# Instance norm on one core: middle units twice as wide, stored in 64 KB rows

## The chip, the core and the metric

The kernel runs on one core of a Trainium2 chip. A core has five engines with a sequencer each: TensorE (PE in the profile), VectorE (DVE), ScalarE (ACT), GpSimd (POOL) and SyncE (SP). SP computes nothing here; it issues DMA transfers. Transfers issued by SP and by ACT go through two queues (q1 and q10 in the profile), and both queues are worked off by the same 16 DMA engines. On-chip memory has 128 partitions. The metric is the device time in microseconds (us) of one execution, as a median of several runs. A trace comes from one profiled execution; its times count from the start of the span.

## The reference

`x` has the shape 4 x 8 x 16 x 256 x 256 in float32 and `gamma` 8 x 16. Each of the 512 channels (4 images times 128 channels) of 256 x 256 values is normalised by itself:

```python
def reference(x, gamma):
    mu = x.mean(axis=(3, 4), keepdims=True)
    var = ((x - mu) ** 2).mean(axis=(3, 4), keepdims=True)
    x_norm = (x - mu) / np.sqrt(var + 1e-5)
    out = x_norm * gamma[None, :, :, None, None]
    return out.astype(np.float32)
```

134.2 MB are read and 134.2 MB are written, each byte once.

## The kernel before

The input, taken as one flat array, is cut into 32 units of 16 channels, numbered 0 to 31. A channel of 65,536 values lies on 8 partitions (S = 8), so a unit is a tile of 128 partitions x 8192 values: 4 MB, 32 KB in each partition, contiguous in DRAM. There are six slots of that size on the chip (`slots`, the tile `xt`), and unit u uses slot u modulo 6.

Setup. VectorE clears a small tile `touch`, and GpSimd stores it over the first 512 bytes of the 16 channels of unit 0's output (line 54), which unit 0's own store overwrites later. GpSimd loads gamma as one row (line 55). The loads of units 0 to 5 are issued at once: units 1 and 3 on ACT's queue, the others on SP's (lines 56 and 57). Sixty NOPs on ACT stand in the source (line 60). GpSimd builds `navg`, a 128 x 128 matrix that holds -1/65536 in 8 x 8 blocks on the diagonal: as a matmul it sums the 8 partitions of each channel and gives the negative mean to all 8 (lines 66 to 76). VectorE and TensorE spread gamma to one column per group of 16 channels (lines 83 to 94), since unit u has the gammas of group u modulo 8.

The loop over the units (lines 105 to 136) is written in order, and every engine works off its own instructions in that order. For each unit: VectorE sums the tile along its rows (line 107), ScalarE sums its squares (line 108, the squares themselves go to `junk`, which nobody reads), TensorE combines both over the partitions of a channel (line 116), then a short chain goes from VectorE (line 117) to ScalarE (the root, line 121) and back to VectorE (reciprocal and gamma, lines 125 and 127). VectorE then normalises the tile in place (line 130). ACT issues the store (line 134), so ACT's next square stands behind that issue. SP issues the load of unit u + 6 into the slot that the store empties (line 136, issued at line 48), and waits for the store to land before it does so.

What sets the order is the two queues and the semaphores alone. The planner keeps the written order. It hands eight semaphores for completed transfers round, in the order in which transfers of both queues are written, so a transfer is issued only once the transfer eight places before it has landed. In the old kernel that made store 27 wait for load 28.

Of the kernel before, what the change touches and what calls it, by code (L numbers as in the profile page):

```python
# [1 line left out]

# [4 lines left out]

F32 = mybir.dt.float32
U8 = mybir.dt.uint8
ALU = mybir.AluOpType  # L10
ACTF = mybir.ActivationFunctionType
AX = mybir.AxisListType


@with_exitstack
def kernel(
    ctx: ExitStack,
    tc: tile.TileContext,
    x: bass.AP,
    gamma: bass.AP,  # L20
    out: bass.AP,
):
    nc = tc.nc
    B, G, C, H, W = x.shape
    P = nc.NUM_PARTITIONS
    HW = H * W
    n_ch = B * G * C
    S = 8
    K = P // S
    F = HW // S  # L30
    U = n_ch // K
    NG = (G * C) // K
    AHEAD = 6
    assert HW % S == 0 and (G * C) % K == 0

    xv = x.rearrange("b g c h w -> (b g c h w)").rearrange("(u p f) -> u p f", p=P, f=F)
    ov = out.rearrange("b g c h w -> (b g c h w)").rearrange("(u p f) -> u p f", p=P, f=F)
    gv = gamma.rearrange("g c -> (g c)")

    data = ctx.enter_context(tc.tile_pool(name="data", bufs=1))  # L40
    singles = ctx.enter_context(tc.tile_pool(name="singles", bufs=1))
    psum = ctx.enter_context(tc.tile_pool(name="psum", bufs=4, space=bass.MemoryType.PSUM))
    ctx.enter_context(tc.manual_schedule())

    slots = [data.tile([P, F], F32, name=f"xt{i}") for i in range(AHEAD)]

    def load(u, queue):
        queue.dma_start(out=slots[u % AHEAD][:], in_=xv[u])  # L48


    g_row = singles.tile([1, G * C], F32, name="g_row")
    touch = singles.tile([16, 128], F32, name="touch")
    nc.vector.memset(touch[:], 0.0)  # L53
    nc.gpsimd.dma_start(out=ov[0][0::S, 0:128], in_=touch[:])  # L54
    nc.gpsimd.dma_start(out=g_row[:], in_=gv[None, :])  # L55
    for u in range(AHEAD):
        load(u, nc.scalar if u in (1, 3) else nc.sync)

    for _ in range(60):
        nc.scalar.nop()  # L60

    eps_t = singles.tile([P, 1], F32, name="eps_t")
    nc.gpsimd.memset(eps_t[:], 1e-5)
    one = singles.tile([1, 1], F32, name="one")
    nc.gpsimd.memset(one[:], 1.0)
    navg = singles.tile([P, K, S], F32, name="navg")
    nc.gpsimd.memset(navg[:], -1.0 / HW)  # L67
    nc.gpsimd.affine_select(  # L68
        out=navg[:], in_=navg[:], pattern=[[-S, K], [0, S]], compare_op=ALU.is_ge,
        fill=0.0, base=0, channel_multiplier=1,  # L70
    )
    nc.gpsimd.affine_select(  # L72
        out=navg[:], in_=navg[:], pattern=[[S, K], [0, S]], compare_op=ALU.is_ge,
        fill=0.0, base=S - 1, channel_multiplier=-1,
    )
    navg_w = navg[:].rearrange("p k s -> p (k s)")
    root_eps = singles.tile([P, 1], F32, name="root_eps")
    nc.scalar.activation(out=root_eps[:], in_=eps_t[:], func=ACTF.Sqrt)  # L78
    g_rep = singles.tile([1, NG, K, S], F32, name="g_rep")
    g_ps = psum.tile([P, NG], F32, name="g_ps", bufs=1)  # L80
    g_col = singles.tile([P, NG], F32, name="g_col")

    nc.vector.tensor_copy(  # L83
        out=g_rep[:],
        in_=g_row[:].rearrange("o (n k) -> o n k", n=NG).unsqueeze(3).to_broadcast([1, NG, K, S]),
    )
    for n in range(NG):
        nc.tensor.matmul(  # L88
            out=g_ps[:, n : n + 1],
            lhsT=g_rep[:, n].rearrange("o k s -> o (k s)"),  # L90
            rhs=one[:],
            start=True, stop=True,
        )
    nc.vector.tensor_copy(out=g_col[:], in_=g_ps[:])  # L94

    junk = singles.tile([P, F], U8, name="junk")

    st = singles.tile([P, U, 2], F32, name="st")
    nvar = singles.tile([P, U], F32, name="nvar")
    std = singles.tile([P, U], F32, name="std")  # L100
    rstd = singles.tile([P, U], F32, name="rstd")
    scale = singles.tile([P, U], F32, name="scale")

    squares = []
    for u in range(U):
        t = slots[u % AHEAD]
        nc.vector.reduce_sum(out=st[:, u, 0:1], in_=t[:], axis=AX.X)  # L107
        square = nc.scalar.activation(  # L108
            out=junk[:], in_=t[:], func=ACTF.Square, accum_out=st[:, u, 1:2],
        )  # L110
        if u:

            tc.declare_no_dep(square.ins, squares[-1].ins, reason="junk, ordered by the root between")
        squares.append(square)
        ps = psum.tile([P, 2], F32, name="ps")
        nc.tensor.matmul(out=ps[:], lhsT=navg_w, rhs=st[:, u], start=True, stop=True)  # L116
        nc.vector.tensor_scalar(  # L117
            out=nvar[:, u : u + 1], in0=ps[:, 0:1], scalar1=ps[:, 0:1],
            scalar2=ps[:, 1:2], op0=ALU.mult, op1=ALU.add,
        )  # L120
        nc.scalar.activation(  # L121
            out=std[:, u : u + 1], in_=nvar[:, u : u + 1], func=ACTF.Sqrt,
            bias=eps_t[:], scale=-1.0,
        )
        nc.vector.reciprocal(out=rstd[:, u : u + 1], in_=std[:, u : u + 1])  # L125
        g = u % NG
        nc.vector.tensor_mul(  # L127
            out=scale[:, u : u + 1], in0=rstd[:, u : u + 1], in1=g_col[:, g : g + 1],
        )
        nc.vector.tensor_scalar(  # L130
            out=t[:], in0=t[:], scalar1=ps[:, 0:1], scalar2=scale[:, u : u + 1],
            op0=ALU.add, op1=ALU.mult,
        )
        nc.scalar.dma_start(out=ov[u], in_=t[:])
        if u + AHEAD < U:
            load(u + AHEAD, nc.sync)


# [1 line left out]
_INS = ['x', 'gamma']  # L140
_OUTS = [((4, 8, 16, 256, 256), 'float32')]


# [23 lines left out]
```

## Time and profile before

| What | Value |
|---|---|
| median of 3 runs | 626.96 us (626.79 to 627.2) |
| span of the profiled execution | 624.9 us |
| first load lands | 22.6 us |
| last load lands | 585.24 us |
| last store issued, landed | 600.32 us, about 623.9 us |
| busy share of VectorE, ScalarE, TensorE | 71%, 38%, 3% |
| moved by DMA | 268.46 MB, mean 430 GB/s |
| steady period of a load and a store | 19.35 us |

The profiled execution has no time of its own beside the span; the three timed runs lie about 2 us above it. A row of busy tenths gives 40 equal slices of the span. A group line gives the line, engine, operation and shapes, then busy time and mean duration in ns of one, then the idle time before it and what ended that. A line of waits gives who waited for whom, the total in us, how often, and the longest. A DMA issue line ends with the median time from issue to landing.

### The profile page before, as it was taken

What the parts mean: (1) busy time and instruction counts of PE and PEld (TensorE: products, weight loads), DVE (VectorE), ACT (ScalarE), POOL (GpSimd) and SP (SyncE); (2) the same over time, 40 slices, a digit from 0 to 9 for tenths busy, and PEclk for the clock granted to TensorE, in tenths of its full rate; (3) what the DMA queues carried; (4) which work ended last, traced back from release to release, by engine and by line L of the source; (5) the groups of instructions that cost most, each with busy time, mean ns of one, the idle gap of its engine ahead of it and who ended that gap; (6) DMA issues with size and microseconds to landing.
All of it is one profiled execution on the core that took longest, in us unless ns stands there. A gap on an engine that the chain in (4) does not pass through costs nothing.

```text
span 624.9 us, 631 instructions
## 1 busy us (share of the span) xinstructions
PE 21.4 (3%) x80; PEld 19.5 (3%) x80; DVE 443.4 (71%) x163; ACT 238.8 (38%) x98; POOL 2.4 (0%) x11
## 2 busy tenths in 40 slices
PE   0200000000000000000000000000000000000000
PEld 0200000000000000000000000000000000000000
DVE  0588999999776687666786767867668676687730
ACT  0444444444443234432344423444224442244400
POOL 1000000000000000000000000000000000000000
DMA  8999999999999999999999999999999999999998
GB/s 370 436 426 430 422 434 436 436 436 437 432 424 433 436 436 424 436 436 434 436 436 432 422 436 436 434 426 436 436 434 436 436 434 419 436 436 434 426 436 369
DMA packets 9282, 268.46 MB, mean 430 GB/s; under 512 B 1072, under 2 KB 1088, under 8 KB 1088
## 3 DMA queue, kind: packets, MB, share of 16 engines
q10 hardware_dynamic: 4896, 142.61, 52.9%
q1 hardware_dynamic: 4320, 125.83, 46.8%
q0 software_dynamic: 64, 0.01, 0.0%
q14 instruction: 2, 0.02, 0.0%
HBM read 134.22 MB, written 134.23 MB: 430 GB/s over the span
## 4 chain that ended last, share of the span: by engine, by line
another core or an unknown queue 61%; DMA 17%; DVE 15%; SPq 1%; PE 1%; issue 0%; ACT 0%
DVE st L107 10%; DMA xt<-in_x_dram 10%; DMA out_dram<-xt 8%; DVE xt L130 5%; SPq L48 1%; PE ps L116 1%; ACT std L121 0%; DVE nvar L117 0%; DVE rstd L125 0%; DVE scale L127 0%
## 5 line engine op out<-in xcount | busy, mean ns | idle before, releaser
L107 DVE TENSOR_REDUCE st<-xt 128x1 f32<-128x8192 f32 x32 | 277.9, 8685 | 100.4 <-DMA xt<-in_x_dram 100.4
L108 ACT ACTIVATE junk<-xt 128x8192 uint8<-128x8192 f32 x32 | 225.0, 7030 | 275.1 <-DMA xt<-in_x_dram 231.9
L130 DVE TENSOR_SCALAR xt<-xt,ps,scale 128x8192 f32<-128x8192 f32 x32 | 145.6, 4550 | 1.2
L121 ACT ACTIVATE std<-nvar,eps_t 128x1 f32<-128x1 f32 x32 | 9.4, 294 | 79.6 <-DVE nvar L117 79.6
L116 PE MATMUL ps<-st,navg 128*128 128x2 f32 x64 | 17.9, 349 | 557.1 <-DVE st L107 557.1
L116 PEld LDWEIGHTS ps<-st,navg 128*128 128x128 f32 x64 | 16.0, 311 | 558.9 <-issue 558.9
L117 DVE TENSOR_SCALAR nvar<-ps 128x1 f32<-128x1 f32 x32 | 9.2, 287 | 23.8 <-PE ps L116 23.8
L125 DVE RECIPROCAL rstd<-std 128x1 f32<-128x1 f32 x32 | 5.2, 164 | 11.6 <-ACT std L121 11.6
L83 DVE COPY g_rep<-g_row 1x1024 f32<-1x1024 f32 x1 | 0.7, 681 | 14.3 <-DMA g_row<-in_gamma_dram 14.3
L108 ACT ACTIVATION_READ_ACCUMULATOR junk<-xt 128x1 f32 x32 | 6.0, 186 | 0.0
L127 DVE TENSOR_TENSOR scale<-rstd,g_col 128x1 f32<-128x1 f32 x32 | 5.1, 159 | 1.1
L88 PE MATMUL g_ps<-one,g_rep 1*128 1x1 f32 x16 | 3.5, 347 | 16.1 <-DVE g_rep L83 16.1
L88 PEld LDWEIGHTS g_ps<-one,g_rep 1*128 1x128 f32 x16 | 3.5, 325 | 16.1 <-issue 16.1
L94 DVE COPY g_col<-g_ps 128x8 f32<-128x8 f32 x1 | 0.2, 166 | 3.7 <-PE g_ps L88 3.7
L78 ACT ACT_TABLE_LOAD x1 | 1.3, 1283 | 1.7 <-PEq L151 1.7
L53 DVE MEMSET touch<- 16x128 f32 x1 | 0.2, 165 | 0.9 <-PEq L151 0.9
L54 POOL DMA_DIRECT2D out_dram<-touch x1 | 0.6, 619 | 0.8 <-DVE touch L53 0.8
L55 POOL DMA_DIRECT2D g_row<-in_gamma_dram x1 | 0.5, 487 | 0.0
L68 POOL TENSOR_SCALAR_AFFINE_SELECT navg<-navg 128x128 f32<-128x128 f32 x1 | 0.4, 400 | 0.1
L72 POOL TENSOR_SCALAR_AFFINE_SELECT navg<-navg 128x128 f32<-128x128 f32 x1 | 0.4, 399 | 0.1
L67 POOL MEMSET navg<- 128x128 f32 x1 | 0.2, 232 | 0.0
L78 ACT ACTIVATE root_eps<-eps_t 128x1 f32<-128x1 f32 x1 | 0.2, 203 | 0.0
(6 smaller groups left out, 0.6 us busy)
## 6 DMA issues: line engine op xcount, KB each, us to landing
out_dram<-xt ACTq DMA_DIRECT2D x32, 4096.0 KB, 62.5
xt<-in_x_dram SPq DMA_DIRECT2D x30, 4096.0 KB, 38.5
xt<-in_x_dram ACTq DMA_DIRECT2D x2, 4096.0 KB, 31.5
out_dram<-touch POOLq DMA_DIRECT2D x1, 8.0 KB, 9.1
g_row<-in_gamma_dram POOLq DMA_DIRECT2D x1, 0.5 KB, 13.3
```

Source lines behind the costliest of these rows:

```text
L48: queue.dma_start(out=slots[u % AHEAD][:], in_=xv[u])
L78: nc.scalar.activation(out=root_eps[:], in_=eps_t[:], func=ACTF.Sqrt)
L83: nc.vector.tensor_copy(out=g_rep[:], in_=g_row[:].rearrange("o (n k) -> o n k", n=NG).unsqueeze(3).to_broadcast([1, NG, K, S]),)
L88: nc.tensor.matmul(out=g_ps[:, n : n + 1], lhsT=g_rep[:, n].rearrange("o k s -> o (k s)"), rhs=one[:], start=True, stop=True,)
L107: nc.vector.reduce_sum(out=st[:, u, 0:1], in_=t[:], axis=AX.X)
L108: square = nc.scalar.activation(out=junk[:], in_=t[:], func=ACTF.Square, accum_out=st[:, u, 1:2],)
L116: nc.tensor.matmul(out=ps[:], lhsT=navg_w, rhs=st[:, u], start=True, stop=True)
L117: nc.vector.tensor_scalar(out=nvar[:, u : u + 1], in0=ps[:, 0:1], scalar1=ps[:, 0:1], scalar2=ps[:, 1:2], op0=ALU.mult, op1=ALU.add,)
L121: nc.scalar.activation(out=std[:, u : u + 1], in_=nvar[:, u : u + 1], func=ACTF.Sqrt, bias=eps_t[:], scale=-1.0,)
L125: nc.vector.reciprocal(out=rstd[:, u : u + 1], in_=std[:, u : u + 1])
L127: nc.vector.tensor_mul(out=scale[:, u : u + 1], in0=rstd[:, u : u + 1], in1=g_col[:, g : g + 1],)
L130: nc.vector.tensor_scalar(out=t[:], in0=t[:], scalar1=ps[:, 0:1], scalar2=scale[:, u : u + 1], op0=ALU.add, op1=ALU.mult,)
```

## The change

The flat array is now cut into 22 units, numbered 0 to 21. The first six and the last six are as before: 16 channels, 8 partitions each, 4 MB. The ten in the middle (units 6 to 15) are wide: 32 channels, 4 partitions each, 128 partitions x 16384 values, 8 MB, 64 KB in each partition. The six slots become three pairs of slots, each pair one tile; a wide unit fills a pair.

A wide unit is loaded by two transfers, one for each half of its columns. Each moves rows of 32 KB that lie 64 KB apart in DRAM, one after the other on SP's queue. Each half is summed and squared when it is there, and the two matmuls add up in one accumulator. The wide unit is normalised by one instruction and stored by one transfer with rows of 64 KB. A list `behind` says which loads are issued behind the store of which unit: unit 6 behind store 1, unit 7 behind store 3, unit 8 behind store 5, each of units 9 to 15 behind the store of the unit three before it, units 16 and 17 behind store 13, 18 and 19 behind store 14, 20 and 21 behind store 15. Each load still waits for the store that held its slot.

For the wide units there is a second averaging matrix (4 x 4 blocks) and a second set of gamma columns, made in the setup. `touch`, its store and the NOPs are gone.

```diff
-    AHEAD = 6
+    SLOTS = 6
+    ENDS = 6
...
-    slots = [data.tile([P, F], F32, name=f"xt{i}") for i in range(AHEAD)]
+    pairs = [data.tile([P, 2, F], F32, name=f"xt{i}") for i in range(SLOTS // 2)]
+    units = []
+    at = 0
+    slot = 0
+    total = n_ch // K
+    while at < total:
+        wide = 2 if ENDS <= at < total - ENDS else 1
+        units.append((at, wide, slot))
+        at += wide
+        slot = (slot + wide) % SLOTS
+    U = len(units)
+
+    def on_chip(u):
+        at, wide, slot = units[u]
+        pair = pairs[slot // 2]
+        if wide == 2:
+            return pair[:].rearrange("p t f -> p (t f)")
+        return pair[:, slot % 2]
+
+    def in_dram(flat, u):
+        at, wide, slot = units[u]
+        return flat[at * K * HW : (at + wide) * K * HW].rearrange("(p f) -> p f", p=P)
 
     def load(u, queue):
-        queue.dma_start(out=slots[u % AHEAD][:], in_=xv[u])
-    touch = singles.tile([16, 128], F32, name="touch")
-    nc.vector.memset(touch[:], 0.0)
-    nc.gpsimd.dma_start(out=ov[0][0::S, 0:128], in_=touch[:])
+        wide = units[u][1]
+        for h in range(wide):
+            queue.dma_start(
+                out=on_chip(u)[:, h * F : (h + 1) * F],
+                in_=in_dram(xf, u)[:, h * F : (h + 1) * F],
+            )
...
+    for u in range(U):
+        free += held[u]
+        while nxt < U and held[nxt] <= free:
+            free -= held[nxt]
+            behind[u].append(nxt)
+            nxt += 1
...
-    for _ in range(60):
-        nc.scalar.nop()
...
+    for wide in (1, 2):
+        s = S // wide
+        k = K * wide
+        ng = GC // k
+        m = singles.tile([P, k, s], F32, name=f"navg{wide}")
...
-        nc.vector.reduce_sum(out=st[:, u, 0:1], in_=t[:], axis=AX.X)
-        square = nc.scalar.activation(
-            out=junk[:], in_=t[:], func=ACTF.Square, accum_out=st[:, u, 1:2],
-        )
+        for h in range(wide):
+            part = t[:, h * F : (h + 1) * F]
+            nc.vector.reduce_sum(out=st[:, u, 2 * h : 2 * h + 1], in_=part, axis=AX.X)
+            square = nc.scalar.activation(
+                out=junk[:], in_=part, func=ACTF.Square, accum_out=st[:, u, 2 * h + 1 : 2 * h + 2],
+            )
...
+            nc.tensor.matmul(
+                out=ps[:], lhsT=navg[wide], rhs=st[:, u, 2 * h : 2 * h + 2],
+                start=h == 0, stop=h == wide - 1,
+            )
...
-        nc.scalar.dma_start(out=ov[u], in_=t[:])
-        if u + AHEAD < U:
-            load(u + AHEAD, nc.sync)
+        nc.scalar.dma_start(out=in_dram(of, u), in_=t)
+        for v in behind[u]:
+            load(v, nc.sync)
```

## The prediction

> **What bounds the kernel now.** I read the page first: the rows over time and the queues.
>
> ```profile
> span 624.9 us, 631 instructions
> DVE  0588999999776687666786767867668676687730
> DMA  8999999999999999999999999999999999999998
> GB/s 370 436 426 430 422 434 436 436 436 437 432 424 433 436 436 424 436 436 434 436 436 432 422 436 436 434 426 436 436 434 436 436 434 419 436 436 434 426 436 369
> DMA packets 9282, 268.46 MB, mean 430 GB/s; under 512 B 1072, under 2 KB 1088, under 8 KB 1088
> q10 hardware_dynamic: 4896, 142.61, 52.9%
> q1 hardware_dynamic: 4320, 125.83, 46.8%
> ```
>
> The DMA row is full from end to end, and the two queues' packets fill 99.7% of the 16 engines' time. VectorE, the busiest engine, stands at 71%. A queue holds 144 packets per transfer of 4 MB (4320 over 30 loads): 128 rows of 32 KB and 16 completions. So a packet here is one row.
>
> Next the waits of the DMA queues, and the DMA issues.
>
> ```profile
> SPq L48 <- DMA out_dram<-xt: 534.4, 26, 59.5
> ...
> out_dram<-xt ACTq DMA_DIRECT2D x32, 4096.0 KB, 62.5
> xt<-in_x_dram SPq DMA_DIRECT2D x30, 4096.0 KB, 38.5
> out_dram<-touch POOLq DMA_DIRECT2D x1, 8.0 KB, 9.1
> g_row<-in_gamma_dram POOLq DMA_DIRECT2D x1, 0.5 KB, 13.3
> ```
>
> SP waits 534 us for stores to free slots, yet always has a second load queued: a load takes 38.5 us from issue to landing, two periods. The small rows matter most: 8 KB took 9.1 us, the time of some seven 32 KB rows. A queue with little to move waits while the other queues' rows pass whole.
>
> Then the chain of waits (start, duration), the store issues over time, and the groups.
>
> ```profile
> 159.62 0.33 SPq L48
> 546.69 0.03 issue
> 546.72 38.51 DMA xt<-in_x_dram
> 585.26 8.70 DVE st L107
> 595.73 4.55 DVE xt L130
> ```
>
> ```profile
> 503.49 0.34 ACTq L134 DMA_DIRECT2D out_dram<-xt  x1
> 527.20 0.34 ACTq L134 DMA_DIRECT2D out_dram<-xt  x1
> 600.32 0.34 ACTq L134 DMA_DIRECT2D out_dram<-xt  x1
> ```
>
> ```profile
> L107 DVE TENSOR_REDUCE st<-xt 128x1 f32<-128x8192 f32 x32 | 277.9, 8685 | 100.4 <-DMA xt<-in_x_dram 100.4
> L108 ACT ACTIVATE junk<-xt 128x8192 uint8<-128x8192 f32 x32 | 225.0, 7030 | 275.1 <-DMA xt<-in_x_dram 231.9
> L130 DVE TENSOR_SCALAR xt<-xt,ps,scale 128x8192 f32<-128x8192 f32 x32 | 145.6, 4550 | 1.2
> ```
>
> Twenty load issues between 159.62 and 546.69 give a period of 19.354 us for a load and a store: 9.677 per transfer, 1.205 per row on each engine and about 0.04 per completion. 64 x 9.677 = 619.3; only 5.6 us of the span are start and end. The last load lands at 585.24, its store is issued 15.08 us later, and all that time stores 28, 29 and 30 (29 us) keep the engines full. That cover is what I watch.
>
> **The change part by part.** The sum goes against the span of 624.9; the median of 626.96 lies 2.06 above it.
>
> Fewer transfers: 22 stores for 32. Ten completions at 0.04: -0.4 us. Whether a 64 KB row is cheaper per byte the trace can't show. Bounds: nothing, or the middle's stores (20 of the 64 transfers) at the best slice's 437 GB/s instead of the period's 8.389 MB / 19.354 us = 433.4: 0.8% of 193.5, -1.6. I take -0.4, since only the completions go away with certainty.
>
> Column halves: a load row is still 32 KB, now 64 KB from the next. Nothing shows this; bounds nothing, and the slowest inner slice (419 against 436, 3.9%) over 20 x 9.677: +7.5. I take nothing, because each row stays one contiguous packet. The Trainium skill, "DMA: Bandwidth & Descriptors", Latency and other measured facts, has copies slowing at large power-of-two pitches (207 GB/s at 512 KiB against 214 full); at 3% the halves would cost an estimated 6 us. No run here shows it, and this pitch is an eighth of that.
>
> Setup: touch and its DMA go. Store 0 waited on it, but it had landed by 10.5 us and the store was issued at 37.68: nothing. Had it warmed the store path, its loss would fall on store 0; stepping through the first rounds below misses the trace by 1.2 us, so +/-1.2, and I take 0. The 60 NOPs have no record, and the table load starts at 1.72, straight behind ACT's two DMA issues: 0. A second averaging matrix costs POOL 1.0 (0.23 + 0.40 + 0.40) at about 4 us, idle time. The second gamma column costs a copy of 0.68, half of L88's 3.5 and a copy of 0.17 behind 19.9 us, so VectorE is free near 22.9 rather than at 22.6: 0.3 late, hidden since store 0 waits behind load 3 on ACT's queue until about 42. Without cover it is 0.3.
>
> Wide units: 32 reductions and 32 squares as before; ten chains of small operations fewer, about 1.75 each on VectorE, which has slack. Normalise: 2 x 4.55 = 9.1. From a second half's landing to its store: 8.70 + 1.75 + 9.1 = 19.6 us instead of 15.1. ACT waits that out with the next square queued behind; squares at 7.2 catch up with reductions at 8.7. SP still has 30 issues, ACT 24 instead of 34. The issues also wait on each other eight back (store 27 was issued 4.4 us late, as load 28 landed); in the schedule below those transfers have landed in time.
>
> **The turn.** A wide store puts rows of 64 KB against loads of 32 KB. If engines take turns by row, stores get two bytes for one of the loads: eight turns of 2.41 + 1.205 = 28.9 us move a whole 8 MB store and only one 4 MB half. Both queues having equal rows, before can't show this directly; by bytes the gap would be nil. I take rows, as the 9.1 us of the 8 KB store is nearest. The Trainium skill, "DMA: Bandwidth & Descriptors", Queues, rings and completion order, says each engine round-robins between queues and finishes a packet before switching. Its typical packet of 9 to 17 descriptors isn't what the trace has (a row each), but with packet equal to row it says the same, and would make turns by bytes wrong.
>
> I stepped the whole schedule by these numbers: data starts 1.3 us after the issue, landing shows 0.95 after the last row, engines alternate, slots free as the diff has it. For the old kernel this gives the last load at 584.0, its store issued at 599.0 and landed at 622.7; the trace has 585.24, 600.32 and 623.9 (600.32 + 23.6). It is 1.2 early throughout. For the new one, unshifted:
>
> - Until 158 nothing differs (stores 4 and 5 land at 138.6 and 158.0). Then wide stores take 31 to 32 us from issue to landing and run ahead of the loads.
> - Wide stores 13, 14 and 15 land at 450.5, 494.0 and 523.0; each releases two of the last six loads.
> - At 523.0 all 26 units of 4 MB before the last six are out, but the rest of load 17 and loads 18 to 21 are still to come. From here rows are equal: they land at 527.9, 544.8, 564.1, 583.5 and 602.9. Each narrow store follows its load by 15.1 and shares with the next.
> - At 602.9 only store 20 is left (issued 598.5, its data ends by 611.7). Store 21 is issued at 602.9 + 15.1 = 618.0 and starts at 619.3: the engines stand idle for 7.6 us. It lands at 602.9 + 15.1 + 1.3 + 9.68 + 0.95 = 629.9.
>
> Against 622.7 that is +7.1 to +7.2, the -0.4 included. Shifting one input at a time (row time, latencies, mid chain by a few tenths) gives +7.1 to +8.4. I take +7.6: span 632.5, time 634.6.
>
> With turns by bytes, store 15 lands at 535.1 with three loads left; they land at 554.5, 573.8 and 593.2. Stores 19 and 20 (19.4 us) then cover 15.1 + 1.3, and the end is 622.3.
>
> **The rivals.**
> - Turns by bytes: -0.4, 626.5. For it: two queues with equal rows share evenly to the last digit. Against: the 8 KB store.
> - The change doesn't do what it says, 64 KB rows being sent as two packets of 32 KB: the same 626.5. For it: every packet so far is at most 32 KB. A wide store would then show 272 packets instead of 144.
> - Faster: 64 KB rows move at the best slice's rate in the middle, -1.6, 625.3. It decides only where the tail stays covered, that is where no more than three loads are left as store 15 lands. Against: stores alone (604 to 622 us) and loads alone (4 to 36 us) run at 430 and 427 GB/s, so neither direction has a faster mode. By the Trainium skill, "DMA: Bandwidth & Descriptors", Specifications, the fabric's ceiling is 435 GB/s; the period's 433.4 agrees and leaves little.
> - The strided halves are slow: up to +7.5 on the forecast, 642. Against: the row length and the packet count are unchanged.
>
> **How the numbers follow.** Turns by row 0.70, by itself 632.0 to 637.5 (7.1 to 8.4, and 1.2 either way for touch and 64 KB rows). Turns by bytes 0.11, split rows 0.09, faster 0.06, slow halves 0.04. A measurement can tell about 0.2% (1.25 us) from no change: faster 0.06, same 0.20, slower 0.74. The range reaches from the two even cases to the top of the likeliest: 626.0 to 637.5; faster and slow halves are left out.
>
> **What would show it.** Right: q10 with 3456 packets (24 x 144); wide stores landing about 31 us after issue and the two halves further apart than their sizes; the last load near 604; a last slice or two of GB/s well below 369 with a gap of 7 to 8 us before the last store. Wrong: last load near 594 and no gap; or middle slices below 430. I would be wrong most simply if the engines share by bytes.

## The result

The changed kernel takes 668.2 us (median of four runs, 664.07 to 670.11) against 626.88 us for the kernel before in the same rounds: a ratio of 1.0649, 95% interval [1.0618, 1.0681]. The forecast was 634.6 with a range of 626.0 to 637.5. The direction was right; the loss is 41 us instead of 8. The changed kernel also scatters by 0.5% either way, the old one by 0.03%. (Where a kernel's runs lie more than 1.5% above its fastest, the ratio leaves them out and the median does not.)

The profiled execution took 666.68 us. The page, for the rows that were shown of before:

```profile
span 665.0 us, 591 instructions
...
DMA  9999999999999999999999999999999999999665
GB/s 378 442 410 432 424 438 442 430 422 426 335 361 347 323 442 452 405 447 416 430 412 396 424 404 428 436 410 386 422 426 442 416 422 396 430 434 440 300 277 252
DMA packets 7811, 268.47 MB, mean 404 GB/s; under 512 B 896, under 2 KB 896, under 8 KB 896
...
q10 hardware_dynamic: 3456, 142.61, 52.2%
q1 hardware_dynamic: 4320, 125.83, 44.8%
```

A slice is 16.6 us. There are three losses: four slices of 323 to 361 GB/s (166 to 233 us) in which the DMA row still says 9, a middle that hovers below the old 433, and three slices of 252 to 300 at the end with the engines partly idle. q10 has the 3456 packets that were forecast for rows sent whole.

The stretches of the trace say the same with sharper edges. Columns: stretch, its length, busy time of each engine with its instructions, granted clock, the share of time in which the DMA engines have a packet, and GB/s. First the kernel before, then the changed one:

```profile
159.00:228.00 69.00, 2.23 (x8) 2.00 (x8) 50.93 (x20) 29.66 (x12) 0.00 (x0) 1.00 1.00 433
228.00:440.00 212.00, 6.13 (x22) 5.51 (x22) 151.84 (x53) 81.29 (x32) 0.00 (x0) 1.00 1.00 434
```

```profile
40.00:158.00 118.00, 4.47 (x16) 4.02 (x16) 101.63 (x32) 56.81 (x22) 0.00 (x0) 1.00 1.00 430
159.00:228.00 69.00, 1.12 (x4) 1.00 (x4) 26.80 (x6) 14.54 (x5) 0.00 (x0) 1.00 1.00 350
228.00:440.00 212.00, 6.14 (x22) 5.52 (x22) 144.21 (x35) 80.11 (x28) 0.00 (x0) 1.00 1.00 423
440.00:634.00 194.00, 5.01 (x18) 4.50 (x18) 130.00 (x38) 66.16 (x25) 0.00 (x0) 1.00 0.95 404
634.00:664.00 30.00, 0.56 (x2) 0.50 (x2) 13.85 (x5) 7.42 (x3) 0.00 (x0) 1.00 0.67 287
```

From 159 to 228 us, while the first two wide stores run, the engines are full (1.00) but move 350 instead of 433 GB/s. So the packets themselves take longer. Only from 440 on is the share below 1.

Issues with the median time to landing, and the end of the chain of waits:

```profile
xt<-in_x_dram SPq DMA_DIRECT2D x30, 4096.0 KB, 52.4
out_dram<-xt ACTq DMA_DIRECT2D x12, 4096.0 KB, 26.9
...
out_dram<-xt ACTq DMA_DIRECT2D x10, 35.6
```

```profile
637.81 8.70 DVE st L159
...
648.28 4.55 DVE xt L183
```

Loads take 52.4 us (38.5 before): the stores run ahead of them, as forecast. The last load lands at 637.81 (585.24 before, forecast near 604), and its store goes out 15.05 us later, at 652.86, after the engines have run dry.

**An account by packets.** The trace also has a record of each packet: queue, start, duration, bytes. The tables below are my own sums over these records. At full speed a row of 32 KB takes 1.213 us and one of 64 KB 2.418. A row's excess is its time above that; the column also holds the completions, 9 ns each on record. All in us for each of the 16 engines, counted from the first data packet (at 1.8 us of the span) to the last:

| | stretch | rows at full speed | slow rows' excess | idle | last load ends at |
|---|---|---|---|---|---|
| before | 621.8 | 621.1 | 1.9 | -1.2 | 581.9 |
| changed | 661.8 | 620.4 | 24.7 | 16.7 | 634.4 |

The loss of 40.0 us is 22.8 of slow rows and 17.9 of idle time, less 0.7 because a row of 64 KB takes 0.3% less than two of 32 KB. Of the slow rows' 24.7, 12.5 are the 64 KB rows of 159 to 228 us alone (241 of the 256 rows of the first two wide stores are slow). Of the idle 16.7, some 9 fall after the last load has landed and some 8 before; 6.6 of these 8 lie between 612.6 us, when the first of the engines lands its part of that load, and 637.8, when the last one does.

### The profile page after: what moved, and what is told of

Same layout as the page of the kernel before. It is cut to its first block, busy times and chain, and to the rows that moved or that the text cites. A ratio compares the mean times of both kernels' runs of the same rounds, so it can differ in the third digit from the quotient of the medians.

```text
span 665.0 us, 591 instructions
## 1 busy us (share of the span) xinstructions
PE 23.3 (3%) x88; PEld 21.3 (3%) x88; DVE 434.0 (65%) x124; ACT 235.9 (35%) x88; POOL 3.1 (0%) x13
## 3 DMA queue, kind: packets, MB, share of 16 engines
q10 hardware_dynamic: 3456, 142.61, 52.2%
## 4 chain that ended last, share of the span: by engine, by line
DVE 41%; DMA 30%; another core or an unknown queue 24%; PE 1%; ACT 1%; issue 1%; SPq 0%
DVE st L159 26%; DMA xt<-in_x_dram 18%; DVE xt L183 14%; DMA out_dram<-xt 12%; PE ps L166 1%; ACT std L174 1%; DVE nvar L170 1%; SPq L73 0%; DVE rstd L178 0%; DVE scale L180 0%
## 5 line engine op out<-in xcount | busy, mean ns | idle before, releaser
L183 DVE TENSOR_SCALAR xt<-xt,ps,scale 128x8192 f32<-128x8192 f32 (+1 forms) x22 | 142.8, 6490 | 0.8
L166 PE MATMUL ps<-st,navg 128*128 128x2 f32 x64 | 17.9, 349 | 612.0 <-DVE st L159 612.0
L174 ACT ACTIVATE std<-nvar,eps_t 128x1 f32<-128x1 f32 x22 | 6.5, 294 | 58.3 <-DVE nvar L170 58.3
L170 DVE TENSOR_SCALAR nvar<-ps 128x1 f32<-128x1 f32 x22 | 6.3, 288 | 16.4 <-PE ps L166 16.4
L178 DVE RECIPROCAL rstd<-std 128x1 f32<-128x1 f32 x22 | 3.6, 164 | 7.9 <-ACT std L174 7.9
L135 PE MATMUL g_ps<-one,g_all 1*128 1x1 f32 x24 | 5.4, 348 | 11.9 <-DVE g_all L130 11.9
L135 PEld LDWEIGHTS g_ps<-one,g_all 1*128 1x128 f32 x24 | 5.3, 324 | 12.0 <-issue 11.3
L180 DVE TENSOR_TENSOR scale<-rstd,g_col 128x1 f32<-128x1 f32 x22 | 3.5, 159 | 0.7
## 6 DMA issues: line engine op xcount, KB each, us to landing
xt<-in_x_dram SPq DMA_DIRECT2D x30, 4096.0 KB, 52.4
```

What stands on the lines that cost most here:

```text
L135: nc.tensor.matmul(out=g_ps[:, n : n + 1], lhsT=g_rep[:, n].rearrange("o k s -> o (k s)"), rhs=one[:], start=True, stop=True,)
L166: nc.tensor.matmul(out=ps[:], lhsT=navg[wide], rhs=st[:, u, 2 * h : 2 * h + 2], start=h == 0, stop=h == wide - 1,)
L170: nc.vector.tensor_scalar(out=nvar[:, u : u + 1], in0=ps[:, 0:1], scalar1=ps[:, 0:1], scalar2=ps[:, 1:2], op0=ALU.mult, op1=ALU.add,)
L174: nc.scalar.activation(out=std[:, u : u + 1], in_=nvar[:, u : u + 1], func=ACTF.Sqrt, bias=eps_t[:], scale=-1.0,)
L180: nc.vector.tensor_mul(out=scale[:, u : u + 1], in0=rstd[:, u : u + 1], in1=g_cols[wide][:, g : g + 1],)
L183: nc.vector.tensor_scalar(out=t, in0=t, scalar1=ps[:, 0:1], scalar2=scale[:, u : u + 1], op0=ALU.add, op1=ALU.mult,)
```

## The experiments

Edits are against the changed kernel unless another is named; "wide" is 2 for a wide unit. The first theory after the result was that something about the wide store's rows is slow in itself: their length, their distance in DRAM, or the strided halves.

**Place and length of the rows.**

```diff
 e1: wide stores in two column halves (32 KB rows, 64 KB apart)
-        nc.scalar.dma_start(out=in_dram(of, u), in_=t)
+        for h in range(wide):
+            nc.scalar.dma_start(
+                out=in_dram(of, u)[:, h * F : (h + 1) * F], in_=t[:, h * F : (h + 1) * F],
+            )
 e2: only the first 60 KB of each wide row, rows 64 KB apart
+            L = 15360
+            nc.scalar.dma_start(out=in_dram(of, u)[:, :L], in_=t[:, :L])
 e3: the same 60 KB, rows 60 KB apart
+            rows = of[at * K * HW : at * K * HW + P * L].rearrange("(p f) -> p f", p=P)
+            nc.scalar.dma_start(out=rows, in_=t[:, :L])
```

> The changed kernel, but a wide unit is stored in two column halves, as it is loaded: rows of 32 KB, 64 KB apart, two transfers. In the changed kernel's trace the first two wide stores (160 to 233 us) have rows of 64 KB that take about 3.2 us instead of 2.42, and the loads beside them pass one 4 MB half per 8 MB store. Theory A (the place: 16 engines writing rows that lie 64 KB apart, in step, are slow whatever the rows' length): store rows of 32 KB over 1.21 us by a third, time 640 to 655. Theory B (the length: a row of 64 KB is what is slow and what takes the longer turn): all rows at 1.21 us, even turns, last load lands near 594, time 626 to 628.

> The changed kernel, but of each 64 KB row of a wide unit only the first 60 KB are stored (a sixteenth of the wide units' output is left out, 5.2 MB or 12 us of DMA); rows still start 64 KB apart. Theory A (place): rows over their share of 2.27 us (60/64 of 2.42) by a third in the first wide stores, time 650 to 660. Theory B (length): the same, 650 to 660. It is the control of the next kernel.

> As the kernel before it in this set, 60 KB of each row of a wide unit stored, but the rows lie 60 KB apart in DRAM, without gaps, so the engines' rows no longer start a power of two apart (the output is at other places, and 12 us of DMA are left out). Theory A (place): rows at 2.27 us, no slow stretch, only the tail of late loads is left: 615 + 8 = 620 to 625. Theory B (length): no different from the kernel with rows 64 KB apart, 650 to 660.

| | time | ratio to before |
|---|---|---|
| e1, stores in halves | 627.66 | 1.0009 [0.9999, 1.0018] |
| e2, 60 KB rows 64 KB apart | 661.41 | 1.0547 [1.0526, 1.0569] |
| e3, 60 KB rows 60 KB apart | 660.88 | 1.0539 [1.0507, 1.0571] |

e1 has the wide units, strided halves in both directions, second matrix, the waits and the missing touch, and is as fast as the kernel before. So all of the loss comes with storing a wide unit as one transfer of 64 KB rows, and the column halves cost nothing. e1 changes two things at once, the length of the rows and the size of the transfer; e5 below takes them apart. e2 and e3 agree: the distance of the rows doesn't matter, and rows that move 6% less of the wide output remain slow.

**Other pairs of row lengths.** In e5 the wide store stays one transfer, each row sent as two pieces of 32 KB. In e6 all pieces are halved (loads and narrow stores 16 KB, wide stores 32 KB). In e7 wide loads are one transfer of 64 KB rows. e9 and e10 are the kernel before with the pieces of one direction cut to 16 KB.

```diff
 e5
+        nc.scalar.dma_start(out=in_dram(of, u), in_=t, max_dma_last_dim=32768)
 e6: also on each load max_dma_last_dim=16384
+        nc.scalar.dma_start(out=in_dram(of, u), in_=t, max_dma_last_dim=16384 * wide)
 e7
+        queue.dma_start(out=on_chip(u), in_=in_dram(xf, u))
 e9, in the kernel before
+        queue.dma_start(out=slots[u % AHEAD][:], in_=xv[u], max_dma_last_dim=16384)
 e10, in the kernel before
+        nc.scalar.dma_start(out=ov[u], in_=t[:], max_dma_last_dim=16384)
```

> The changed kernel with every wide store still one transfer of 8 MB, but sent as two 32 KB pieces per row. Theory B (a piece over 32 KB is what is slow): no slow piece, even turns, the same as with two stores per unit, 626 to 628. If the transfer of 8 MB were the trouble, and not its rows: 660 to 670.

> The changed kernel with every row cut in half: loads and narrow stores in pieces of 16 KB, wide stores in pieces of 32 KB. The turns are as uneven as in the changed kernel (two bytes stored for one loaded while wide stores run), but no piece is over 32 KB. Theory B1 (a piece over 32 KB is slow by itself): pieces at 1.21 and 0.61 us, and only the prediction's step is left, late loads at the end with about 7.6 us of idle engines: 633 to 637. Theory B2 (uneven turns are what slows the stores, whatever the length): wide store pieces a third over 1.21 us, 655 to 670.

> The changed kernel with wide loads in one transfer with rows of 64 KB as well, so turns are even and half a unit is never there early. Theory B1 (over 32 KB is slow by itself): stores, perhaps loads too, over 2.42 us, 650 to 690. Theory B2 (uneven turns): rows at 2.42 us; the late halves alone cost little, 626 to 640.

> The kernel before, narrow units alone, but every load goes in pieces of 16 KB beside stores of 32 KB: uneven turns with nothing else changed. Theory T (turns by piece): two bytes stored for one loaded, loads fall behind, and the same stepping as in the prediction gives 12.4 us of idle engines at the end and 1.5 us for the smaller pieces: 639 to 643. If the engines share by bytes, or the uneven turn only matters with pairs of slots: 626 to 629.

> The mirror image: stores in pieces of 16 KB beside loads of 32 KB, so that loads run ahead and the stores are what is left at the end, when they need nothing but the engines. Theory T: no idle, 1.5 us for the smaller pieces, 627 to 629.5. If uneven turns cost engine time by themselves (stores slowed beside longer rows): 635 or more.

| | store / load piece, KB | time | ratio to before | excess | idle |
|---|---|---|---|---|---|
| e5 | 32 / 32, store of 8 MB | 637.86 | 1.0167 [1.0146, 1.0188] | 7.3 | 5.5 |
| e6 | 32 / 16 in the middle | 652.61 | 1.0369 [1.0311, 1.0427] | 8.8 | 14.0 |
| e7 | 64 / 64 in the middle | 636.99 | 1.0157 [1.0137, 1.0177] | 7.8 | 4.0 |
| e9 | 32 / 16 throughout | 653.14 | 1.0384 [1.0327, 1.0441] | 10.3 | 14.9 |
| e10 | 16 / 32 throughout | 636.22 | 1.0146 [1.0112, 1.0179] | 4.5 | 4.1 |

In e5 the rows have 32 KB and the store is still one of 8 MB: some 30 us of the loss are gone, and some 11 us remain while the transfer stays one of 8 MB. The time lies in neither of its two ranges, and the same holds for e6 and e9; e10 hits the range for uneven turns that cost engine time by themselves, and e7 the one for even turns.

e9 shows the turn by itself, in a kernel without any 64 KB row. Its issues:

```profile
out_dram<-xt ACTq DMA_DIRECT2D x32, 4096.0 KB, 19.8
xt<-in_x_dram SPq DMA_DIRECT2D x30, 4096.0 KB, 79.2
```

Equal transfers of 4 MB, but stores land in 19.8 us and loads in 79.2 (62.5 and 38.5 before): the queue with pieces twice as long runs ahead. It is as slow as e6, with much the same split of excess and idle time. Every combination of pieces that I tried, other than transfers of 4 MB in rows of 32 KB both ways, was slower.

**How many wide units.** One constant.

```diff
 e4: -    ENDS = 6
     +    ENDS = 14     (two wide units)
 e11: -    ENDS = 6
      +    ENDS = 2     (fourteen wide units)
```

> The changed kernel with 14 narrow units at each end, so two wide units only. If each wide store in step costs its slow rows, two of them cost 8 rows x 0.8 us each, some 13 us, and no late loads remain at the end, since 14 narrow units follow: 636 to 642. If the loss comes from late loads behind stores alone (the prediction's tail) nothing is left: 626 to 628.

> The changed kernel with two narrow units at each end instead of six, so 14 wide units. Stepping the schedule gives no late loads at the end (the pairs fall differently): idle near nothing. If the slow rows go by the number of wide stores, 14/10 of 22.8 us is 32: 655 to 662. If the idle stretch at the end comes from engines drifting apart and not from late loads, it stays at 15 us or grows: 670 to 680.

e4 took 650.01 us (1.0366 [1.0299, 1.0432]), e11 655.83 (1.0440 [1.0404, 1.0476]). Stretches of e4, then of e11:

```profile
40.00:314.00 274.00, 8.93 (x32) 8.02 (x32) 212.27 (x72) 116.05 (x46) 0.00 (x0) 1.00 1.00 432
314.00:382.00 68.00, 1.12 (x4) 1.01 (x4) 31.96 (x10) 14.83 (x6) 0.00 (x0) 1.00 1.01 361
382.00:600.00 218.00, 6.13 (x22) 5.50 (x22) 154.70 (x56) 84.00 (x34) 0.00 (x0) 1.00 1.00 429
```

```profile
40.00:190.00 150.00, 5.03 (x18) 4.52 (x18) 112.72 (x29) 63.69 (x23) 0.00 (x0) 1.00 1.00 431
190.00:440.00 250.00, 6.70 (x24) 6.01 (x24) 173.97 (x38) 94.36 (x32) 0.00 (x0) 1.00 1.01 432
440.00:585.00 145.00, 3.91 (x14) 3.51 (x14) 80.56 (x19) 43.62 (x15) 0.00 (x0) 1.00 0.99 413
585.00:602.00 17.00, 0.56 (x2) 0.50 (x2) 8.97 (x2) 7.19 (x3) 0.00 (x0) 1.00 0.37 156
```

Two wide units cost 23 us. 15.6 us an engine are slow rows, 10.0 of them the two wide stores' own: both are slow for nearly their whole length (2.95 and 3.14 us a row), at 314 us instead of 159, so the moment in the kernel is not the cause. The other 5.0 are idle; I had expected none, because my steps for this kernel were wrong, not because of the chip (redone by the forecast's own rules they give an estimated 6 to 8). With fourteen wide units the rows run at 2.42 to 2.48 us and 431 to 432 GB/s for 400 us; I had expected slow rows there; that the time still falls into the range expected for them, 655 to 662, is luck. Its loss is idle time above all (21.1 us of it against 10.0 of slow rows), half of it at 585 to 602, where the engines have a packet for 37% of the time. So "64 KB rows beside 32 KB rows" is not slow as such, and the loss has two parts that come and go separately.

**The row's price without the kernel.** e8 and e12 do nothing but transfers: phases, one after the other, of 32 MB out of one tile and 32 MB into two others, 64 KB or 32 KB rows.

```diff
 e8, phases (store KB, load KB):  32/-  64/-  32/32  64/32  64/64  32/64  32/16
 e12, phases of 64/32: loads from the stores' places; the same, with VectorE
   and ScalarE at work on the stored tile; loads from 24 MB ahead; from 16 MB
   ahead; then 64/- and 32/32 with the engines at work
```

> No normalisation at all: seven phases, one behind the other, each of which stores 32 MB from one tile and, in the last five, loads 32 MB beside it. Rows in KB (store, load): 32 alone; 64 alone; 32 and 32; 64 and 32; 64 and 64; 32 and 64; 32 and 16. Theory B1: store rows of 64 KB take over 2.42 us in all their phases, the alone one too. Theory B2: only where the rows are unequal, that is also 32 beside 16. A third, C: only beside loads, because a long row of one engine stands against other engines' loads; then 64 alone runs at 430 GB/s and 64 beside 32 or 64 does not. By turns by row, 64 beside 32 moves two bytes out for one in, 32 beside 64 one for two.

> Six phases as in the phases before, no normalisation, stores of 64 KB rows beside loads of 32 KB rows: (1) loads and stores at the same offset, (2) the same with VectorE's sums and ScalarE's squares running over the stored tile, (3) loads three units of 8 MB further on than the stores, (4) two further on, as in the changed kernel, (5) 64 KB stores alone with the sums and squares, (6) 32 KB beside 32 KB with them. Theory D1 (compute on the tile slows a long row and throws engines out of step): rows over 2.42 us in phases 2 and 5 alone. Theory D2 (the place of loads against stores in DRAM): phases 3 and 4 alone, at about 3.3 us. Neither: all at 2.42 us.

In e8, 64 KB rows took 2.42 us alone and 2.418 to 2.44 beside 32 KB loads, at 430 GB/s. That phase's 32 MB of stores took 124.7 us from the signal to the last landing, where equal shares of 433 GB/s would need 155: the stores got close to two bytes for each of the loads (524 load rows begun beside 512 store rows of twice the length). VectorE's wait for those stores:

```profile
458.13 0.06 DVE L52 MEMSET src<- 128x1 f32 x1 [124.67 <-DMA out_dram<-src]
```

In e12 the same work as in e8's fourth phase was slow in the first phase and nearly full speed in the second:

```profile
22.00:164.00 142.00, 0.00 (x0) 0.00 (x0) 0.00 (x0) 1.00 0.99 349
209.00:332.00 123.00, 82.33 (x10) 36.90 (x11) 0.00 (x0) 1.00 0.99 417
```

The engines at work (82 and 37 us in the second row) do no harm, and loads from other places (2.55 and 2.68 us a row) lie between the two. Yet the first row's 349 GB/s is all but the 350 of the changed kernel at 159 to 228. Something decides between 2.42 and 3.0 us for the same rows.

**Engines out of step?** In the changed kernel the 16 engines, which land a transfer within 0.4 to 0.5 us of each other until the first wide store, drift 18 us apart by 400 us and up to 43 later. I took that for the cause. e13 puts half of the engines one row behind by a store of 8 rows ahead of phases 3, 5 and 6; e14 puts all behind alike by 16 rows; e15 lets loads and stores go together (phases 1, 3, 5) or 8.7 or 17.4 us apart (2, 4 and 6).

```diff
 e13 (e14: [0:16, 0:F])
+        nc.scalar.dma_start(out=rows(of, 16 - len(kicks))[0:8, 0:F], in_=src[0:8, 0:F])
 e15, between the signal that lets the loads go and that for the stores
+        for _ in range(later):
+            nc.vector.reduce_sum(out=st[:, 0:1], in_=src[:, 0:F], axis=AX.X)
```

> No normalisation: seven phases, one after the other, each with 32 MB out beside 32 MB in; phases 1 to 5 have 64 KB store rows beside 32 KB load rows, phases 6 and 7 have 32 KB both ways. Ahead of phases 3, 5 and 6 stands a store of 8 rows of 32 KB, which should reach only 8 of the 16 engines, one row each, and put them 1.2 us behind the others. Theory (engines out of step slow the long rows, whatever put them out of step): phases 3 and 5 slow, that is four stores in about 140 to 148 us with a mean 64 KB row of 2.8 to 3.1 us; phases without the kick are a matter of how they happen to start, fast (125 us, 2.42 us) where their first rows start within 1 us of each other, slow where not; phases 6 and 7 (equal rows) full speed, 1.21 us a row, about 155 us for both ways, kick or no kick. Rival 1 (the slow state belongs to a place in memory): phases 1 and 4 (same places) are alike, 2 and 5 are alike, whatever the kick. Rival 2 (the slow state is a matter of the moment on the chip): no pattern with the kick.

> As the kernel with the kick of 8 rows, but the store ahead of phases 3, 5 and 6 has 16 rows, one for each engine, so that all engines are put behind alike. Theory: the kick does nothing to the step of the engines, phases 3 and 5 are like phases 1, 2 and 4, fast (125 us, 2.42 us) where the first rows start together; a phase 3 or 5 that is slow here as often as with 8 rows speaks against the theory. Rival 1: as before, by place. Rival 2: no pattern.

> No normalisation: seven phases of 32 MB out beside 32 MB in, phases 1 to 6 with 64 KB store rows beside 32 KB load rows, phase 7 with 32 KB both ways. In phases 1, 3 and 5 loads and stores are let go within half a microsecond, in 2 and 4 the stores one sum of 8.7 us behind the loads, in 6 two sums. In the three phase kernels so far the first phase was slow (3.01 to 3.07 us a 64 KB row, loads and stores 2.3 us apart, the 16 engines in step) and all later ones less so (2.42 to 2.68 us, 5 to 28 us apart). Theory A (loads and stores that begin together run over the same rows and get in each other's way): phases 1, 3 and 5 at 2.9 to 3.1 us, phases 2, 4 and 6 at 2.42 to 2.7. Theory B (what comes first in a kernel is slow): phase 1 alone near 3.0, phases 2 to 6 all at 2.42 to 2.7. Phase 7 at 1.21 to 1.25 by both.

The theory fell, and so did both of e15's. A 64 KB row's mean by phase: e13 3.01, 2.58, 2.67, 2.47, 2.51; e14 3.07, 2.49, 2.47, 2.61, 2.57; so the kicked phases 3 and 5 are not the slow ones. Phases 1 and 4, at the same places, differ by 0.5 us. In e15:

```profile
22.00:164.00 142.00, 0.00 (x0) 0.00 (x0) 1.00 0.99 350
219.00:361.00 142.00, 0.00 (x0) 0.00 (x0) 1.00 0.99 350
395.00:538.00 143.00, 0.00 (x0) 0.00 (x0) 1.00 0.99 350
593.00:734.00 141.00, 0.06 (x1) 0.00 (x0) 1.00 0.99 353
768.00:911.00 143.00, 0.00 (x0) 0.00 (x0) 1.00 0.99 352
974.00:1118.00 144.00, 0.06 (x1) 0.00 (x0) 1.00 0.97 380
```

The first five phases are all slow, with the engines' first rows within 0.4 to 0.65 us of each other: engines in step are slow here. (In the sixth the first rows lie 1.65 us apart, and a row takes 2.74 on average.) In e11 they were in step as well and fast. The pattern that was left is in the order of the rows. A transfer of 128 rows is 8 rows for each engine. I counted, at the start of each store row, how many load rows an engine had begun, less the store rows begun before it: the loads' lead, taken modulo 8. At a lead of 1, an engine loads row r of a transfer just before it stores row r of another. In e15 the phases with a start apart had a lead of 9, which is 1 again.

**The lead, set on purpose.** e16 lets both go together and has 0, 64, 0, 32, 128 and 96 rows loaded first, to set the lead. e18 repeats that with 0, 16 and 112 (phases 1, 4 and 5), and turns the order of the rows in DRAM alone, for the stores in phase 2 and for the loads in phase 3.

```diff
 e16, and e18 in phases 4 and 5
+        if lead:
+            nc.sync.dma_start(
+                out=dst[1][0:lead, F:], in_=rows(xf, 15)[0:lead, F:], max_dma_last_dim=32 * 1024,
+            )
 e18, in phases 2 and 3, for the DRAM side
+        return rows(flat, u).rearrange("(b a) f -> a b f", a=16)
```

> No normalisation: six phases of 32 MB out in rows of 64 KB beside 32 MB in in rows of 32 KB, loads and stores let go within half a microsecond. A transfer is 8 rows for each of the 16 engines. Ahead of the loads of phases 2, 4, 5 and 6 stands one more load of 64, 32, 128 and 96 rows: 4, 2, 8 and 6 rows for each engine, so that the loads run so many rows behind the stores. Theory C (an engine's rows are slow while it loads row number r of its eight between storing row r and r + 1 of the same eight places): phases 1, 3 and 5 (0, 0 and 8 rows apart, the same numbers) at 2.9 to 3.1 us a 64 KB row, phases 2, 4 and 6 at 2.42 to 2.6. In the kernel with starts 8.7 us apart the loads were 12.7 us, about a whole transfer of 8 rows, ahead, and it was slow too, which fits. Theory D (engines that start within 0.65 us of each other are slow, whatever the rows): all six at 2.9 to 3.1. Against D: with two narrow units at each end the engines were in step from 95 to 127 us and every row took 2.42.

> No normalisation: six phases of 32 MB out beside 32 MB in, loads and stores let go together, loads in rows of 32 KB. Phase 1: 64 KB store rows, nothing else. Phase 2: the store's 128 rows go to DRAM in the order 0, 16, 32 ... 112, 1, 17 ...; on the chip they are taken in the same order as in phase 1. Phase 3: the loads' rows are taken from DRAM in that order instead. Phases 4 and 5: as phase 1 with 16 and 112 rows loaded first, one and seven for each engine. Phase 6: 32 KB rows both ways. Theory C with the partitions as the cause (an engine writes partition p on the chip just before it reads partition p): phases 1, 2 and 3 all at 2.9 to 3.1 us a 64 KB row. Theory C with the places in DRAM as the cause: phase 1 at 3.0, phases 2 and 3 at 2.42 to 2.6. By both: phases 4 and 5 (another row number) at 2.42 to 2.55, phase 6 at 1.21 to 1.25.

The phases of e16, while the stores run:

```profile
22.00:166.00 144.00, 0.06 (x1) 0.00 (x0) 1.00 0.99 350
210.00:328.00 118.00, 0.00 (x0) 0.00 (x0) 1.00 0.99 419
377.00:521.00 144.00, 0.06 (x1) 0.00 (x0) 1.00 0.99 348
567.00:683.00 116.00, 0.00 (x0) 0.00 (x0) 1.00 0.99 429
730.00:844.00 114.00, 0.00 (x0) 0.00 (x0) 1.00 0.99 428
900.00:1023.00 123.00, 0.00 (x0) 0.00 (x0) 1.00 0.99 418
```

Slow with no rows loaded first, both times; fast with 64, 32 and 96. The fifth phase was expected slow (128 rows are a whole transfer) and was fast; by the count its loads had got three rows along before the first store, where those of phase 1 had got one, so its lead is 3 - 8 = -5, which is 3 and not 1. All phases with 64 KB stores beside 32 KB loads and rows in plain order:

| loads' lead, modulo 8 | phases | mean 64 KB row | 32 MB of stores took |
|---|---|---|---|
| 0.6 to 1.0, throughout | 11 (first of e12, e13, e14, e18; five of e15; e16's 1 and 3) | 3.01 to 3.08 us | 141 to 144 us |
| 0 | 2 (e16's 4, e18's 4) | 2.42, 2.43 | 116, 117 |
| 2 to 6 | 4 (e16's 2, 5, 6; e18's 5) | 2.42 to 2.47 | 114 to 123 |
| differs between engines, whose first store rows start 1 to 5 us apart | 13 | 2.42 to 2.74 | 119 to 147 |

Four store transfers of 8 rows, each with a load row, are 32 x (2.418 + 1.213) = 116.2 us: five of the six fast phases, with 114 to 118 us, run at the turns that the forecast assumed; the sixth took 123.

The turned rows told nothing. Turning changed the speed and the lead together: phase 2 fell to 317 GB/s and 3.58 us a row at a lead of 3, phase 3 had 2.53 us at -1 with the loads at 1.70. So whether the clash is on the chip (the same partitions) or in DRAM stays open. The Trainium skill, "DMA: Bandwidth & Descriptors", The descriptor swizzle, gives each engine a fixed set of eight partitions in a transfer of 128; by that an equal row number would be an equal partition, if every transfer takes them in the same order. No run here shows partitions.

The count in the whole kernels, at the start of each wide store:

| | lead | 64 KB row (e2, e3: 60 KB, 2.267 at full speed) |
|---|---|---|
| changed, first two wide stores | 1.0, 0.6 | 3.26, 3.14 |
| changed, other eight | 2.1 to 6.7 | 2.42 to 2.58 |
| e4, both | 1.0, 0.8 | 2.95, 3.14 |
| e11, thirteen beside loads | 0.4, and 1.8 to 7.4 | 2.42 to 2.48 |
| e2 and e3, first two | 1.0, 0.7 to 0.9 | 2.68, 2.86 and 2.97, 2.95 |
| e3, the sixth | 1.1 | 2.65 |
| before, steady, 32 KB rows both ways | 1.0 | 1.213 (32 KB) |

The last row matters: the old kernel runs at a lead of exactly 1.0 for 500 us, at full speed. So the lead alone doesn't make rows slow: at 32 KB both ways it costs nothing. What 64 KB rows both ways would do at a lead of 1 no run shows; in e7 the wide stores start at leads near 0, or from 6 up.

**Does it cost the changed kernel its time?** e17 puts two rows an engine ahead of the first wide store, written over the last unit's output, which its own store writes again later.

```diff
+        if u == ENDS:
+            nc.scalar.dma_start(out=in_dram(of, U - 1)[0:32], in_=t[0:32, 0:F])
         nc.scalar.dma_start(out=in_dram(of, u), in_=t)
```

> The changed kernel with one more store ahead of the first wide store: 32 rows of 32 KB, two for each engine, over the output of the last unit, which that unit's own store writes later. In the changed kernel's trace the first two wide stores stand beside loads whose row number of eight is the store's own (0.6 to 1.0 load rows further than the stores) and took 3.26 and 3.14 us a row; the eight others stand 2 to 6 rows apart and took 2.42 to 2.58. Theory C (rows are slow where an engine loads row r just before it stores row r): two rows of difference bring the first two wide stores to 2.42 to 2.55 us a row; 256 rows on 16 engines at 0.8 us less are 12.5 us an engine, less 2.4 for the two rows, so about 658 us, and as low as 640 if the engines also drift apart less, against the changed kernel's 668.2. Rival (first wide stores are slow whatever the row numbers): 3.1 to 3.3 us a row still, about 670 us.

```profile
164.00:228.00 64.00, 1.68 (x6) 1.51 (x6) 31.23 (x8) 17.25 (x8) 0.00 (x0) 1.00 1.00 419
228.00:440.00 212.00, 5.59 (x20) 5.02 (x20) 142.69 (x33) 72.93 (x26) 0.00 (x0) 1.00 1.00 417
440.00:641.00 201.00, 5.02 (x18) 4.51 (x18) 122.67 (x37) 66.17 (x25) 0.00 (x0) 1.00 0.92 381
```

The first two wide stores now run at a lead of 3.8 and 3.6 and take 2.50 and 2.42 us a row; their stretch moves 419 GB/s instead of 350. The slow rows there are explained and gone. The time hardly follows: six runs from 652.9 to 673.6, median 664.7, ratio 1.0473 [1.0427, 1.0519] from the two lowest. The profiled run is the slowest of the six: later wide stores average up to 2.74 us a row (381 GB/s from 440 to 641), excess is 21.5 us an engine in all, and idle time 24.5. One of its later stores, at a lead of 1.0 in its first half, took only 2.48; the engines are several microseconds apart by then, and the mean lead says little. Of the 12.5 us that I expected to come back (10 with the two rows' own time off), 3.5 did in the median, which is not clear of this kernel's scatter: the rest was lost again further on, in slow rows and idle engines.

The rule of the lead doesn't carry over to engines out of step. The trace names no engine, but a row begins as its engine's last one ends, so the rows can be chained, roughly, engine by engine. In the other eight wide stores of the changed kernel rows at their own engine's lead of 1 are slow (over 2.5 us) in 4% of cases, rows at other leads in 3 to 32%. In e17 it is 42 to 49% at leads of 0 to 2 and 7 to 22% at the others. What makes rows slow there is open.

## Why the prediction was right and wrong

- Turns by row, 0.70, against turns by bytes or split rows: right. The 3456 packets rule out split rows; e8's 124.7 us and e9's 19.8 against 79.2 us show the turns. The Trainium skill, "DMA: Bandwidth & Descriptors", Queues, rings and completion order, has each engine finish a packet before it switches; the traces agree, with a row as the packet.
- "Until 158 nothing differs": right. 430 GB/s to 158 us, store 0 issued at 37.66 (37.68 before), store 5 landed at 159.2.
- Column halves at nothing, setup and touch at nothing: right. e1 holds them all and is at 1.0009. Fewer transfers at -0.4: not shown. The forecast took 40 ns for a completion, and its record lasts 9, so ten are 0.1 us; the 0.7 that the rows at full speed save comes from the longer rows, inside the bounds given for them.
- The uncovered end, 7.6 us: right in kind and nearly in size. The last store follows the last load by 15.05 us, and from that load to the end each engine is idle for 9.1 us on average.
- The step that failed is the sum "eight turns of 2.41 + 1.205 = 28.9 us". It priced both rows at their speed alone and held that price for the whole middle. The first wide store's eight turns took some 34 us (its first row starts at 159.3, the next store's at 193.9). Measured over the kernel a 64 KB row took 2.63 and a 32 KB load row 1.24: 22.8 us an engine more than before. The bounds for 64 KB rows, "-1.6" to nothing, had no loss in them at all, although nothing in the trace of before excluded one; the slowest inner slice, which bounded the column halves at +7.5, belonged here too.
- The second failure lies in the stepped schedule: it moved all 16 engines together. In fact they drifted up to 43 us apart, and a transfer lands with its last engine. That is most of the other 8 us of idle time, before the last load: engines that had done their part of it by 612.6 us had nothing to do while others worked on it until 637.8, where the schedule had it land at 602.9. Why they drift is open; the engines come 8 to 43 us apart in e5, e6, e7, e9 and e10 and in the changed kernel, and no more than 1.1 and 1.6 in the kernel before and in e1.
- A sum that doesn't come out: the range for turns by row, "632.0 to 637.5", is not what its parts give. One 1.2 either way makes it 632.9 to 636.6 (from 626.96, with 7.1 and 8.4), and 1.2 for each of the two, touch and 64 KB rows, 631.7 to 637.8. The measured 668.2 lies far outside of all three.
- The range's top, 637.5, was the top of one mechanism's variants. The faster, even and slow-halves rivals did not come true; the rival that was missing is "unequal rows slow each other".

What is shown: all of the loss comes with the wide store as one transfer of 64 KB rows (e1), some 30 us of it with the rows' length and some 11 that stay while it is one transfer of 8 MB (e5); the stores run ahead two to one; and with the engines in step 64 KB store rows beside 32 KB load rows are slow at a lead of 1 (e16, e18, and the first two wide stores of the changed kernel, of e4 and, undone, of e17). What is not: what inside the chip makes that lead slow, why the load rows slow as well, what makes rows slow once the engines are apart, and what drives the drift. No version beat the kernel before.

## What to carry to other kernels

Where loads and stores share the DMA engines around the clock, give both the same row length and the same transfer size: 4 MB in rows of 32 KB both ways ran at 433 GB/s, and every other combination cost 1.5 to 6.5%, also e7 with equal rows of 64 KB in the middle alone. When one queue's rows are longer, count who gets ahead, how many transfers are left at the end to cover the last chain, and leave room in the range for rows that slow each other. In these traces a wide stretch of GB/s below its neighbours with the DMA share at 1.00 meant slow packets, and a share below 1.00 missing ones; the two need different cures.

## What the runs showed of the hardware that was not expected

- Beside 32 KB load rows and with the engines in step, a 64 KB store row takes 2.42 us or about 3.05, by whether the engine has just loaded the row of the same number: up to 429 against 350 GB/s, slow in 11 phases of 11 at that lead and fast in 6 of 6 at others.
- At the same lead, 32 KB rows both ways run at full speed (1.213 us).
- Longer rows gain nothing: 2.418 us for 64 KB is twice 1.213 less 0.3%.
- Rows 64 KB apart in DRAM cost nothing in either direction (e1).
- With pieces or transfers of unequal size the 16 engines drift apart, by 8 to 49 us in kernels of 636 to 668 us (49 in e2), and the time of one kernel scatters by up to 3% between runs (e17).
